# A hybrid attention trunk in float32: scratch fetches on GpSimd's DMA queue, mixer A's queries and keys a group ahead

## The chip, the cores and the metric

The kernel runs on one core of one Trainium2 chip. The metric is the device time of one execution in microseconds (us). A core has five engines with an instruction queue each: TensorE (PE, with its weight loads shown apart as PEld), VectorE (DVE), ScalarE (ACT), GpSimd (POOL) and SyncE (SP), which here only issues DMAs. An engine takes its instructions in order; one that waits holds up those behind it.

## The reference

One pre-normalised layer of a decoder trunk on 256 tokens of 4096 features. One input projection feeds two mixers and their gates. Cut to what matters here:

```
h = rmsnorm(x, norm_g);  proj = h @ w_in
(q_a, k_a, v_a, z_a, q_b, kc, vc, ksl, vsl, kwn, vwn, z_b, g_b) = split(proj)
o_a = dilated_mixture(q_a, k_a, v_a)          # 16 heads of 128; three (window, dilation) patterns
                                              # merged by their softmax denominators, ALiBi penalty
o_b = nsa(q_b, kc, vc, ksl, vsl, kwn, vwn, sigmoid(g_b))   # 16 heads; compressed, selected and
                                              # window branches, keys and values of 2 groups
y_a = rmsnorm(o_a, out_g_a) * silu(z_a)
y_b = rmsnorm(o_b, out_g_b) * silu(z_b)
out = rmsnorm(x + concat(y_a, y_b) @ w_out, final_g)
```

With 256 tokens, mixer A's three patterns of one head are one softmax over all causal keys, in which a key counts once for each pattern that holds it (the matrix MULT).

## The kernel before, in words

All products are of float32 data in split form. An operand is split into a high part, which ScalarE rounds to the matmul's type, and a low part, which VectorE takes as the difference (`split_to`, lines 102 to 109, recorded at L105 and L106, or L108 and L109 with a scale); a product is then three matmuls (`mm3`, L98 to L100). Nearly all of TensorE's time goes into the two projections.

The work comes in stages. First the input is split and three chunks of the projection (compressed, window and gate columns) are made. Then a stage of paired column chunks makes q, k, v, q_b and more with fewer products (`run_pairs`). Its results are written by GpSimd's DMAs to scratch tensors in DRAM (scr_q, scr_k, scr_v, scr_qb, scr_sel, scr_za). The **middle stage**, which the change touches, has `run_stream` work through eight more chunks: three of z_a, four of z_b, and the first of the output projection. Weights are loaded in pieces of 1 MB through SP's queue (L255), split on ACT and DVE (wh, wl) and multiplied into the accumulators acc. Between these matmuls, small steps of the attention are set: a queue `tasks` of generators, of which `advance` takes one step (to the next `yield`) each time that a credit, counted by k steps of the projection, is full. The tasks are two `compress`, four `attend_a` (mixer A, a group of four heads each), `mixer_done("a")`, `start_b`, four `attend_b`, `mixer_done("b")`, and later the turning of the gated outputs (`turn_y`, L783). After it the output projection follows in pairs, and a last stage ends the kernel.

The order of the instructions in the middle stage isn't the program's. Inside the paired stages a manual schedule keeps the order as written. Elsewhere the framework's planner orders each engine's queue: it plays the program through with its own costs, prefers what comes first in the program, and fills an engine's gaps with later work whose inputs and buffers are free by its reckoning. The chip then runs that fixed order, with semaphores for every dependence.

How data comes back from scratch: `fetch` (L562 to L565) takes a tile with the tag qk, of which there are two buffers, and issues one DMA from SP (L564). Every fetch must so wait until the tile of two fetches before has been read. In `attend_a(hg)`, before the change:

- at its start the values v and queries q of the group are there; `split_values` makes the high and low values (tile va, one of two buffers of the tag n, which kaT shares), then the keys are fetched (L639);
- `divide` (L567 to L570) scales the queries by the tokens' norm on DVE; `transposed` (L588) turns them by TensorE (L601) and splits them (qaT);
- the same for the keys (kaT); then the fetches of the next group's values and queries are issued (L649), or, in the last group, those of sel and kw, which `start_b` uses;
- a pipeline over four heads of three functions, `scores`, `turn` and `values`, two heads apart. `scores` multiplies (s, in PSUM, tag ps with three buffers), applies the distances (n, L663), takes minima (L667), exponentials (L669) and weighted sums (L670). `turn` transposes n (pt, L680) and splits it (pah on ACT, pal on DVE). `values` multiplies with va (L692, L693).

`compress(t, 1)` fetches the first group's values and queries ahead (L843). `evict_away` (L572 to L579) stores kvc, kw and vg to scratch in the first stage, from SP (L578). `mixer_done` (L728 to L759) makes the mixer's norm (rms_of; its power step runs on POOL, L115, names roa and rob), loads the stored gates z by `load` (L741, SP, four buffers of tag zt), applies SiLU and multiplies (L725). `gate_z` stores gates of chunks that come too early (L769, SP). POOL else does the small memsets of kc (L908) and c (L1038) and the stores of the paired stages.

Of the kernel before, what the change touches and what calls it, by code (L numbers as in the profile page):

```python
# [23 lines left out]
HD = 128  # L24
# [59 lines left out]
def hybrid_trunk(ctx: ExitStack, tc: tile.TileContext, a: dict):  # L84
    nc = tc.nc
# [16 lines left out]
    def split_to(h, l, src, scale=None):  # L102

        if scale is None:
            nc.scalar.activation(h, src, AF.Copy)  # L105
            nc.vector.tensor_sub(l, src, h.bitcast(F32))  # L106
        else:
            nc.scalar.activation(h, src, AF.Copy, scale=scale)  # L108
            nc.vector.scalar_tensor_tensor(l, src, scale, h.bitcast(F32), op0=OP.mult, op1=OP.subtract)  # L109
# [442 lines left out]
    st = {}  # L552
# [4 lines left out]
    def scratch(key, width=CW):  # L557
        if key not in scr:
            scr[key] = dram.tile([P, NT, width], F32, name=f"scr_{key}")
        return scr[key]  # L560

    def fetch(key, width=CW):  # L562
        t = room["zq"].tile([P, NT, width], F32, name="fetched", tag="qk", bufs=2)
        nc.sync.dma_start(t, scratch(key))  # L564
        return t  # L565

    def divide(t):  # L567

        for m in range(NT):
            nc.vector.tensor_scalar_mul(t[:, m], t[:, m], rstd[:, m : m + 1])  # L570

    def evict_away(key, width=CW):  # L572

        def done(ps):
            t = room["ev"].tile([P, NT, width], F32, name="away", tag="ev", bufs=3)
            for m in range(NT):
                nc.scalar.activation(t[:, m], ps[m][:, :width], AF.Copy, scale=rstd[:, m : m + 1])
            nc.sync.dma_start(scratch(key, width), t)  # L578
        return done  # L579

    def split_values(src):

        v = room["work"].tile([P, NT, 4, 2, HD], F32R, name="va", tag="n", bufs=2)
        for m in range(NT):
            split_to(v[:, m, :, 0], v[:, m, :, 1], src[:, m].rearrange("p (j d) -> p j d", j=4), rstd[:, m : m + 1])
        return v

    def transposed(src, key, scale=None):  # L588

        if key == "ka":  # L590
            hl = room["work"].tile([P, 2, 4, SEQ], F32R, name="kaT", tag="n", bufs=2)
            h, l = hl[:, 0], hl[:, 1]
        else:
            h = room["work"].tile([P, 4, SEQ], F32R, name=key + "Th", tag="qTh", bufs=1)
            l = room["work"].tile([P, 4, SEQ], F32R, name=key + "Tl", tag="qTl", bufs=1)
        for pair in range(2):
            pt = room["psm"].tile([P, 2, NT, P], F32, name="pt", tag="ps")
            for j in range(2):
                for m in range(NT):
                    hh = 2 * pair + j  # L600
                    nc.tensor.transpose(pt[:, j, m], src[:, m, hh * HD : (hh + 1) * HD], ident)  # L601
            split_to(h[:, 2 * pair : 2 * pair + 2].rearrange("p a b -> p (a b)"),
                     l[:, 2 * pair : 2 * pair + 2].rearrange("p a b -> p (a b)"),
                     pt.rearrange("p a b c -> p (a b c)"), scale)
            yield
        st[key + "T"] = (h, l)
# [10 lines left out]
    def o_at(which, c0, n):  # L617
        q, at = divmod(c0, DH // 2)
        return o_tiles(which)[q][:, :, at : at + n]
# [7 lines left out]
    def pipeline(units, stages, at):  # L627

        for t in range(len(units) + at[-1]):
            for f, d in reversed(list(zip(stages, at))):  # L630
                if 0 <= t - d < len(units):
                    f(units[t - d])
            yield
            yield

    def attend_a(hg):
        vsrc, qsrc = st.pop("va"), st.pop("qa")
        v = split_values(vsrc)
        ksrc = fetch(f"k{hg}")  # L639
        yield  # L640
        divide(qsrc)
        yield
        yield from transposed(qsrc, "qa", SCALE)
        yield
        divide(ksrc)
        yield
        yield from transposed(ksrc, "ka")
        if hg < 3:
            st["va"], st["qa"] = fetch(f"v{hg + 1}"), fetch(f"q{hg + 1}")  # L649
        else:  # L650
            st["sel"], st["kw"] = fetch("sel"), fetch("kw", 2 * HD)
        qh, ql = st["qaT"]
        kh, kl = st["kaT"]
        o_tiles("a")
        parts = [slice(0, P), slice(P, SPAN)]
        live = {}

        def scores(j):
            s = room["psm"].tile([P, SPAN], F32, name="s", tag="ps")
            mm3(s[:, :P], qh[:, j, :P], ql[:, j, :P], kh[:, j, :P], kl[:, j, :P])  # L660
            mm3(s[:, P:], qh[:, j, P:], ql[:, j, P:], kh[:, j], kl[:, j])
            n = room["zq"].tile([P, SPAN], F32, name="n", tag="zt", bufs=4)
            nc.vector.scalar_tensor_tensor(n, K["DA"], SLOPES[hg * 4 + j], s, op0=OP.mult, op1=OP.subtract)  # L663
            mn = room["work"].tile([P, NT], F32, name="mn", tag="mn", bufs=4)
            den = room["work"].tile([P, NT], F32, name="den", tag="den", bufs=4)
            for m in range(NT):
                nc.vector.tensor_reduce(mn[:, m : m + 1], n[:, parts[m]], axis=AX.X, op=OP.min)  # L667
            for m in range(NT):
                nc.scalar.activation(n[:, parts[m]], n[:, parts[m]], AF.Exp, bias=mn[:, m : m + 1], scale=-1.0)  # L669
                nc.vector.scalar_tensor_tensor(n[:, parts[m]], n[:, parts[m]], 1.0, K["MULT"][:, parts[m]],  # L670
                                               op0=OP.mult, op1=OP.mult, accum_out=den[:, m : m + 1])
            rden = room["work"].tile([P, NT], F32, name="rden", tag="rden", bufs=4)
            nc.vector.reciprocal(rden, den)
            live[j] = (n, rden)

        def turn(j):
            n, rden = live[j]
            pt = room["psm"].tile([P, SPAN], F32, name="pt", tag="ps")
            for b in range(3):
                nc.tensor.transpose(pt[:, b * P : (b + 1) * P], n[:, b * P : (b + 1) * P], ident)  # L680
            live[j] = (*split_psum(pt, SPAN, "pa"), rden)

        def values(j):
            ph, pl, rden = live.pop(j)
            head = hg * 4 + j

            po = room["pso"].tile([P, NT, 2, HD], F32, name="po", tag="po")
            for m, blocks in enumerate([[(0, 0)], [(P, 0), (2 * P, 1)]]):
                out = po[:, m].rearrange("p s d -> p (s d)")
                for at, b in blocks:  # L690
                    vb = v[:, b, j].rearrange("p s d -> p (s d)")
                    nc.tensor.matmul(out, ph[:, at : at + P], vb, start=b == 0, stop=False)  # L692
                    nc.tensor.matmul(out, pl[:, at : at + P], vb, start=False, stop=b == m)  # L693
            t = room["work"].tile([P, NT, 2, HD], F32, name="ot", tag="c3", bufs=1)
            for m in range(NT):
                nc.scalar.activation(t[:, m], po[:, m], AF.Copy, scale=rden[:, m : m + 1])
            nc.vector.tensor_add(o_at("a", head * HD, HD), t[:, :, 0], t[:, :, 1])

        yield from pipeline(range(4), [scores, turn, values], [0, 2, 4])
        square_sums("a", hg)  # L700

    def square_sums(which, hg):
# [26 lines left out]
    def mixer_done(which):  # L729

        rms_of(which)
        finished.add(which)
        loaded = deque()
        todo = list(waiting)
        waiting.clear()

        def load():
            z = todo.pop(0)
            sz = [room["zq"].tile([P, CW], F32, name="sz", tag="zt", bufs=4) for m in range(NT)]
            for m in range(NT):  # L740
                nc.sync.dma_start(sz[m], scratch(f"z{z[0]}{z[1]}")[:, m])  # L741
            loaded.append((z, sz))

        load()
        if todo:
            load()
        for _ in range(3):
            yield
        while loaded:
            z, sz = loaded.popleft()  # L750
            for m in range(NT):
                nc.scalar.activation(sz[m], sz[m], AF.Silu, scale=rstd[:, m : m + 1] if z == ("a", 0) else 1.0)
            yield
            yield from gate(*z, sz)
            if todo:
                load()
            yield
# [75 lines left out]
    def compress(t, which):  # L833
# [6 lines left out]
                nc.tensor.transpose(pt[:, g, m], t[:, m, c0 : c0 + HD], ident)  # L840
        nc.scalar.activation(tT, pt, AF.Copy)
        if which == 1:
            st["va"], st["qa"] = fetch("v0"), fetch("q0")  # L843
        pe, w2 = small.pop(which)
        w2h = room["work"].tile([P, 2, HD], F32R, name="w2h", tag="pTh", bufs=2)
        w2l = room["work"].tile([P, 2, HD], F32R, name="w2l", tag="pTl", bufs=2)
# [610 lines left out]
```

## Time and profile before

| | us |
|---|---|
| median of 3 runs | 1622.27 |
| lowest and highest | 1621.72, 1624.2 |
| the profiled execution | 1622.32 |
| its span, first to last instruction | 1620.5 |
| TensorE busy | 1601.9 |
| VectorE busy | 1368.8 |
| ScalarE busy | 994.6 |
| GpSimd busy | 142.6 |

The granted clock of TensorE is 0.998 of full speed. In a profile, L12 is line 12 of the kernel; an operation is named by engine, line and "out<-in" in the program's tile names; the bracket at the end of a timeline's row tells how long the engine had stood idle before it and which instruction or DMA ended that. SPq is SP's queue. A matmul row's length includes the pipeline's depth, so rows of one engine overlap. Rows of DMAs give the issue; the time to landing stands in the list of DMA issues, a median from issue to landing.

### The profile page before, as it was taken

How to read it: one execution, taken by the hardware profiler on the slowest of the kernel's cores; microseconds unless marked ns; L12 is line 12 of the kernel's file. 1: busy time of each engine (PE TensorE's matmuls, PEld its weight loads, DVE VectorE, ACT ScalarE, POOL GpSimd, SP SyncE). 2: the span in 40 equal slices, each digit the busy share in tenths (PEclk: the TensorE clock that was granted, in tenths of full speed). 3: DMA queues.
4: the chain of work that ended last, by engine and by line, in shares of the span. 5: the costliest groups of instructions: out<-in, count | busy, mean ns of one | idle time of the engine just before them, and what ended most of it. 6: DMA issues, size and time to landing. Idle time of an engine off the chain costs nothing.

```text
span 1620.5 us, 20719 instructions
## 1 busy us (share of the span) xinstructions
PE 1601.9 (99%) x7685; PEld 1326.4 (82%) x7685; DVE 1368.8 (84%) x1596; ACT 994.6 (61%) x1242; POOL 142.6 (9%) x196
## 2 busy tenths in 40 slices
PE   9999999999999999999999999999999999999997
PEld 6998888888888888888887788888888887888887
DVE  8679989898999898989878877788788779989885
ACT  7755656565656565656546666766667655656553
POOL 0000212021212020202000000000000000202110
PEclk9999999999999999999999999999999999999999
DMA  8776888888888888888888555654345556988874
GB/s 336 268 250 208 261 264 260 254 260 266 256 270 259 253 263 262 264 249 262 251 312 306 179 190 193 233 174 143 117 144 189 179 194 211 261 252 259 280 299 169
DMA packets 104565, 384.87 MB, mean 237 GB/s; under 512 B 12496, under 2 KB 13136, under 8 KB 93072
## 3 DMA queue, kind: packets, MB, share of 16 engines
q1 hardware_dynamic: 81792, 332.42, 58.3%
q0 software_dynamic: 22240, 50.08, 13.8%
q8 instruction: 60, 0.98, 0.2%
q10 hardware_dynamic: 432, 1.05, 0.2%
q14 instruction: 41, 0.34, 0.1%
HBM read 334.69 MB, written 50.91 MB: 238 GB/s over the span
## 4 chain that ended last, share of the span: by engine, by line
PE 89%; DVE 6%; issue 2%; DMA 2%; ACT 1%; SPq 0%; ACTq 0%; POOLq 0%; POOL 0%; DVEq 0%
PE p L99 16%; PE p L100 16%; PE p L98 16%; PE acc L99 9%; PE acc L100 9%; PE acc L98 9%; PE e L100 2%; PE e L98 2%; PE e L99 2%; PE ph L875 1%; DVE wl L106 1%; PE pt L1056 1%; DVE bf L443 1%; DMA w<-in_w_in 1%; DVE bp L106 1%
## 5 line engine op out<-in xcount | busy, mean ns | idle before, releaser
L106 DVE TENSOR_TENSOR wl<-w,wh 128x1024 fp32r<-128x1024 f32 (+2 forms) x178 | 207.7, 1171 | 99.4 <-ACT wh L105 98.9
L105 ACT ACTIVATE wh<-w 128x1024 fp32r<-128x1024 f32 (+2 forms) x178 | 180.4, 1017 | 115.3 <-PE acc L100 99.9
L98 PE MATMUL acc<-wh,xh 128*128 128x512 f32 (+2 forms) x640 | 242.7, 379 | 0.6 <-ACT wh L105 0.6
L443 DVE TENSOR_TENSOR bf<-bt,bf 128x2048 fp32r<-128x2048 f32 x106 | 242.1, 2284 | 0.0
L99 PE MATMUL acc<-wl,xh 128*128 128x512 f32 (+2 forms) x640 | 239.7, 375 | 1.3 <-DVE wl L106 1.3
L100 PE MATMUL acc<-wh,xl 128*128 128x512 f32 (+2 forms) x640 | 239.2, 374 | 0.0
L106 DVE TENSOR_TENSOR bp<-bw,bp 128x2048 fp32r<-128x2048 f32 x72 | 164.8, 2288 | 69.5 <-ACT bp L105 69.5
L438 ACT ACTIVATE bf<-bt 128x1024 fp32r<-128x1024 f32 x106 | 112.4, 1060 | 163.0 <-DVE bt L436 162.6
L435 ACT ACTIVATE bf<-bw 128x1536 fp32r<-128x1536 f32 x106 | 157.7, 1488 | 72.2 <-DMA bw<-in_w_in 39.4
L105 ACT ACTIVATE bp<-bw 128x2048 fp32r<-128x2048 f32 x72 | 137.6, 1911 | 94.1 <-PE e L100 78.2
L442 DVE TENSOR_TENSOR bf<-bw,bf 128x1536 fp32r<-128x1536 f32 x106 | 185.6, 1751 | 0.0
L436 DVE TENSOR_TENSOR bt<-bw 128x1024 f32<-128x1024 f32 x106 | 129.5, 1222 | 12.6 <-DMA bw<-in_w_in 7.0
L441 ACT ACTIVATE bf<-bt 128x1024 fp32r<-128x1024 f32 x106 | 112.7, 1063 | 41.8 <-DVE bt L440 38.7
L99 PEld LDWEIGHTS acc<-wl,xh 128*128 128x128 f32 x640 | 120.6, 188 | 20.1 <-DVE wl L106 3.0
L100 PEld LDWEIGHTS acc<-wh,xl 128*128 128x128 f32 x640 | 120.2, 188 | 20.4
L98 PEld LDWEIGHTS acc<-wh,xh 128*128 128x128 f32 x640 | 120.4, 188 | 18.9 <-ACT wh L105 1.1
L98 PE MATMUL p<-bp,xh 128*128 128x512 f32 x324 | 126.0, 389 | 0.0
L99 PE MATMUL p<-bp,xh 128*128 128x512 f32 x324 | 126.0, 389 | 0.0
L100 PE MATMUL p<-bp,xl 128*128 128x512 f32 x324 | 126.0, 389 | 0.0
L99 PE MATMUL p<-bf,sum 128*128 128x512 f32 x320 | 124.7, 390 | 0.0
L98 PE MATMUL p<-bf,sum 128*128 128x512 f32 x320 | 124.6, 390 | 0.0
L100 PE MATMUL p<-bf,sum 128*128 128x512 f32 x320 | 124.5, 389 | 0.0
(327 smaller groups left out, 3373.8 us busy)
## 6 DMA issues: line engine op xcount, KB each, us to landing
bw<-in_w_in SPq DMA_DIRECT2D x288, 512.0 KB, 6.5
w<-in_w_in SPq DMA_DIRECT2D x60, 1024.0 KB, 5.2
bw<-in_w_out SPq DMA_DIRECT2D x96, 512.0 KB, 5.6
w<-in_w_out SPq DMA_DIRECT2D x16, 1024.0 KB, 5.5
scr_q<-parts POOLq DMA_DIRECT2D x30, 256.0 KB, 7.8
scr_k<-parts POOLq DMA_DIRECT2D x30, 256.0 KB, 7.7
scr_v<-parts POOLq DMA_DIRECT2D x30, 256.0 KB, 7.9
scr_qb<-parts POOLq DMA_DIRECT2D x30, 256.0 KB, 8.3
```

Of the source, the lines that this page charges most:

```text
L98: nc.tensor.matmul(out, lh, rh, start=start, stop=False)
L99: nc.tensor.matmul(out, lh, rl, start=False, stop=False)
L100: nc.tensor.matmul(out, ll, rh, start=False, stop=stop)
L105: nc.scalar.activation(h, src, AF.Copy)
L106: nc.vector.tensor_sub(l, src, h.bitcast(F32))
L435: nc.scalar.activation(h[:, :3], w[:, B22:], AF.Copy)
L436: nc.vector.tensor_tensor(t[:, T3 : T1 + 1], w[:, B22 : B11 + 1], w[:, B12 : B12 + 1].to_broadcast([P, 2, CW]), op=OP.subtract)
L438: nc.scalar.activation(h[:, 3:5], t[:, T3 : T1 + 1], AF.Copy)
L441: nc.scalar.activation(h[:, 5:], t[:, T2:], AF.Copy)
L442: nc.vector.tensor_sub(l[:, :3], w[:, B22:], h[:, :3].bitcast(F32))
L443: nc.vector.tensor_sub(l[:, 3:], t, h[:, 3:].bitcast(F32))
L875: nc.tensor.matmul(ph, both, w[:, :, j], start=l == 0, stop=l == CBL - 1)
```

## The change

`fetch`, `evict_away` and the gate loads of `mixer_done` issue from GpSimd's queue instead of SP's. In mixer A, queries and keys are now what is there at a group's start. The group's values are fetched once its queries are transposed, into the queries' buffer; the next group's queries once its keys are transposed. The values are split in the fifth step of the pipeline, and behind that split the next group's keys are fetched, or sel in the last group. The yield behind the key fetch is gone and one stands behind the transposed keys, so a group still has 24 steps.

```diff
@@ fetch
-        nc.sync.dma_start(t, scratch(key))
+        nc.gpsimd.dma_start(t, scratch(key))
@@ evict_away
-            nc.sync.dma_start(scratch(key, width), t)
+            nc.gpsimd.dma_start(scratch(key, width), t)
@@ attend_a
-        vsrc, qsrc = st.pop("va"), st.pop("qa")
-        v = split_values(vsrc)
-        ksrc = fetch(f"k{hg}")
-        yield
+        qsrc, ksrc = st.pop("qa"), st.pop("ka")
         divide(qsrc)
         yield
         yield from transposed(qsrc, "qa", SCALE)
+        vsrc = fetch(f"v{hg}")
         yield
         divide(ksrc)
         yield
         yield from transposed(ksrc, "ka")
         if hg < 3:
-            st["va"], st["qa"] = fetch(f"v{hg + 1}"), fetch(f"q{hg + 1}")
+            st["qa"] = fetch(f"q{hg + 1}")
         else:
-            st["sel"], st["kw"] = fetch("sel"), fetch("kw", 2 * HD)
+            st["kw"] = fetch("kw", 2 * HD)
+        yield
@@ attend_a, its end
-        yield from pipeline(range(4), [scores, turn, values], [0, 2, 4])
+        v = None
+        for n, _ in enumerate(pipeline(range(4), [scores, turn, values], [0, 2, 4])):
+            if n == 4:
+                v = split_values(vsrc)
+                if hg < 3:
+                    st["ka"] = fetch(f"k{hg + 1}")
+                else:
+                    st["sel"] = fetch("sel")
+            yield
         square_sums("a", hg)
@@ mixer_done, load
-                nc.sync.dma_start(sz[m], scratch(f"z{z[0]}{z[1]}")[:, m])
+                nc.gpsimd.dma_start(sz[m], scratch(f"z{z[0]}{z[1]}")[:, m])
@@ compress
         if which == 1:
-            st["va"], st["qa"] = fetch("v0"), fetch("q0")
+            st["qa"], st["ka"] = fetch("q0"), fetch("k0")
```

## The prediction

> **What bounds the kernel now.** First the page's span and busy times, then the shares of the chain of waits:
>
> ```profile
> span 1620.5 us, 20719 instructions
> PE 1601.9 (99%) x7685; PEld 1326.4 (82%) x7685; DVE 1368.8 (84%) x1596; ACT 994.6 (61%) x1242; POOL 142.6 (9%) x196
> PE 89%; DVE 6%; issue 2%; DMA 2%; ACT 1%; SPq 0%; ACTq 0%; POOLq 0%; POOL 0%; DVEq 0%
> ```
>
> TensorE (PE) is busy 1601.9 of 1620.5 us and holds 89% of the chain; no queue that issues DMAs holds a share. The change leaves every matmul as it is, so it can save only time in which PE stands still, and only in the middle stage, where the fetches lie. So I asked for the waits of PE and of its weight loads (PEld) from 810 to 1320 us; columns are total us, times, longest:
>
> ```profile
> PE s L98 <- DVE pal L106: 2.8, 4, 1.1
> PE acc L99 <- DVE wl L106: 0.7, 1, 0.7
> PEld s L98 <- DVE pal L106: 3.7, 4, 1.3
> PEld s L100 <- DVE qbTl L109: 0.6, 2, 0.3
> ```
>
> That is the whole prize. Four stalls before a score matmul of mixer A, one per head group, cost 2.8 us by PE's row and 3.7 us by the weight loads', which see the wait from its start; I use 3.7. One stall at the start of the stage costs 0.7. Together 4.4 us, 0.27% of the time; about 0.2%, or 3.2 us, is what a measurement of this kernel can tell from no change.
>
> Where the four stalls come from is in the timelines of VectorE (DVE), of the DMA issues on SP and of the weight loads:
>
> ```profile
> 947.46 0.55 DVE L663 SCALAR_TENSOR_TENSOR n<-cmat,s 128x384 f32<-128x384 f32 x1 [0.33 <-PE s L100]
> 948.62 0.49 DVE L570 TENSOR_SCALAR fetched<-fetched,rstd 128x512 f32<-128x512 f32 x1 [0.61 <-DMA fetched<-scr_q]
> 949.54 0.48 DVE L570 TENSOR_SCALAR fetched<-fetched,rstd 128x512 f32<-128x512 f32 x1
> 954.56 0.55 DVE L106 TENSOR_TENSOR pal<-pt,pah 128x384 fp32r<-128x384 f32 x1
> ...
> 912.93 0.33 SPq L564 DMA_DIRECT2D fetched<-scr_q  x1
> 944.41 0.33 SPq L564 DMA_DIRECT2D fetched<-scr_q  x1
> 976.74 0.33 SPq L564 DMA_DIRECT2D fetched<-scr_q  x1
> ...
> 916.45 0.49 DVE L570 TENSOR_SCALAR fetched<-fetched,rstd 128x512 f32<-128x512 f32 x1
> 981.17 0.49 DVE L570 TENSOR_SCALAR fetched<-fetched,rstd 128x512 f32<-128x512 f32 x1 [0.83 <-DMA fetched<-scr_q]
> 1011.78 0.87 DVE L570 TENSOR_SCALAR fetched<-fetched,rstd 128x512 f32<-128x512 f32 x2
> ...
> 922.99 0.19 PEld L98 LDWEIGHTS s<-kaT,qaTh 128*128 128x128 f32 x1 [0.48 <-DVE pal L106]
> 955.16 0.19 PEld L98 LDWEIGHTS s<-kaT,qaTh 128*128 128x128 f32 x1 [1.14 <-DVE pal L106]
> 987.71 0.19 PEld L98 LDWEIGHTS s<-kaT,qaTh 128*128 128x128 f32 x1 [1.34 <-DVE pal L106]
> 1019.55 0.19 PEld L98 LDWEIGHTS s<-kaT,qaTh 128*128 128x128 f32 x1 [0.78 <-DVE pal L106]
> ```
>
> In each group the score matmul waits for a PSUM bank that DVE frees with pal, the end of a dense run of softmax work. Into that run, right behind the first n (L663), the planner has set the two divides (L570) of what was just fetched for the next group, as filler. DVE takes its instructions in order, so a fetch that lands late stops the softmax too. The first group has the divides but no wait for a fetch: stall 0.48. The second waits 0.61 more and stalls 1.14 (0.48 + 0.61 = 1.09), the third 0.83 and stalls 1.34 (sum 1.31). So a wait for a fetch at this place passes to PE one for one, while work that the planner knew of (the divides) leaves 0.48 at most. The last group divides sel and stalls 0.78.
>
> **The change part by part.** *Queues.* Some 35 DMAs leave SP for GpSimd (POOL): 20 fetches, 12 loads of gates, 3 stores. SP saves 0.33 us each by the rows above, 11.6 us in all, worth nothing: SP has no share of the chain, and in the stage PE's only wait on split weights is the 0.7. POOL gets the issues; what they cost and when they land show only in DMAs that POOL issues already:
>
> ```profile
> fetched<-scr_q SPq DMA_DIRECT2D x4, 512.0 KB, 3.8
> xr<-in_x POOLq DMA_DIRECT2D x1, 512.0 KB, 5.9
> r<-scr_r POOLq DMA_DIRECT2D x10, 256.0 KB, 8.9
> scr_r<-xr POOLq DMA_DIRECT2D x1, 512.0 KB, 2.9
> ...
> 1219.68 0.69 POOL L115 TENSOR_TENSOR rob<-rsq,nhalf 128x2 f32<-128x2 f32 x1 [25.60 <-DVE rsq L114]
> 1220.54 0.77 POOL L1122 DMA_DIRECT2D xr<-in_x  x1 [0.17 <-DMA sz<-scr_zb]
> ```
>
> A 512 KB load lands 5.9 us after issue from POOL in this very stage, against 3.8 for the queries from SP; the far ends are 8.9 (ten at once) and 2.9 (a store in a quiet moment, so a gain isn't excluded). I take 5.9, the same size, direction and stage: 2.1 us later. [...]
>
> *Mixer A's order.* The arithmetic is the same, and so are the 24 steps of a group (one yield goes with the key fetch, one comes behind the transposed keys). With two fetch buffers, the next group's queries still can't be fetched before this group's keys are transposed: the issue stays where it is (944.41 and its kin), only the landing moves. If the divides stay behind the first n, the landings at 5.9 give waits of 912.93 + 5.9 − 916.45 = 2.4 us, 944.41 + 5.9 − 948.01 = 2.3 (n ends at 947.46 + 0.55) and likewise 2.3, in place of 0, 0.61 and 0.83: 5.6 us more. If they go behind pal, all three stalls go: 0.48 + 1.14 + 1.34 = 3.0 us less. Between these ends I take 0: a planner sets the divides by the landing it assumes, and in the three rows here it missed by 0 to 0.83; I expect a like miss on the other queue. In the last group the sel divide leaves the place (sel is now fetched after the values), worth between 0.78 and 0; but the split of the values comes near the same run in all four groups:
>
> ```profile
> L109 DVE SCALAR_TENSOR_TENSOR va<-fetched,rstd,va x8: 730/743/748, 896.8 to 994.1; 128x512 fp32r<-128x512 f32 x8
> SPq L564 <- DVE va L109: 22.6, 4, 7.2
> ```
>
> Two of these, 1.49 us of DVE a group, move with two ACT copies. It is work that the planner knows of, so it cost at most 0.48 a group if it behaved as the divides did; it could also push the divides out. I set it and the sel divide against each other, 0. The keys' fetch used to wait on SP for that split (22.6 us in four); it now starts in mid-group, and its 2.1 us are hidden by the rest of the group. If that cover failed, the price would be up to 2.1 us in three groups.
>
> *The stage's start and the rest.* Rows from the waits of ACT, SP's and POOL's timelines, and the tile o_b:
>
> ```profile
> ACT w2h L105 <- DMA w<-in_cmp_k_w: 10.5, 1, 10.5
> ACT vB L105 <- DMA fetched<-scr_vg: 2.0, 1, 2.0
> ...
> 827.62 0.38 SPq L564 DMA_DIRECT2D fetched<-scr_kvc  x1
> 1210.06 9.41 SPq L741 DMA_DIRECT2D sz<-scr_zb  x4
> ...
> 832.66 0.12 POOL L908 MEMSET kc<- 128x32 f32 x1 [51.42 <-PE e L100]
> 832.98 0.58 POOL L1304 DMA_DIRECT2D scr_sel<-parts  x1 [0.19 <-issue]
> 1032.95 0.42 POOL L1038 MEMSET c<- 128x384 f32 x1 [197.79 <-DVE o_a L697]
> 173.79 2.32 POOL L461 DMA_DIRECT2D scr_q<-parts  x4 [104.40 <-ACT parts L457]
> ...
> L783 PE MATMUL pt<-ident,o_b x32: 270/272/276, 1257.7 to 1276.3; 128*128 128x128 f32 x32
> ```
>
> At the start, ACT stands 10.5 us for a small weight whose load was issued on SP just behind kvc's 512 KB. With kvc on POOL it lands earlier by some of that transfer; PE's 0.7 stall should go: −0.7. ACT waits 2.0 us for vg; up to 2.1 more, before the 0.6 us of PE waits at L100: I take +0.3, bounds 0 and 2.1. The gate loads of mixer B move behind or beside the rob step on POOL (1219.68): at worst the first starts 9.6 us later and lands 2 us later, while TensorE first turns o_b at 1257.7, some 30 us after: 0. The fetches of qb are a group ahead: 0. Of the three stores, POOL has nothing else to issue until 173.79, and kvc isn't read before 827.62: 0.
>
> The sum is −0.7 + 0 + 0 + 0.3 = −0.4 us, from 1622.32 us for the profiled execution (span 1620.5) to 1621.9. The median of three runs, 1622.27, is 0.05 below that execution, so it stands for the median too.
>
> **The rivals.** *Gain in full:* the divides land behind pal, the sel divide goes, the split values find room. Then 3.7 + 0.7 go: 1617.9. For it: a later landing can drive the filler out of the dense run, and the keys come early. Against: n to pal lasts 7 us (947.46 to 954.56), longer than the 2.1 us by which the landing moves, so the next gap may still be inside it.
>
> *Slower: DVE stops for the later landing.* The divides, or the split values, keep their place. Three waits of 2.3 to 2.4 add 5.6, vg 2.1, the start gives 0.7 back: +7.0, so 1629.3. It decides from a landing later than the assumed one by 1.1 us more than now in each of the three groups (3.2 us in all). For it: the one-for-one rows. [...]
>
> *Slower: POOL's queue.* POOL also takes its work in order; a fetch set behind the memset of c, which stood 197.79 us, or behind rob, starts late. Against: the planner put the memset of kc ahead of stores that come first in the program, so it places by readiness. If it hits one fetch by 7 us with 2 us of cover, +5: 1627.
>
> *The change misses its aim:* SP's queue was never what starved PE, so freeing it does nothing. This is part of my forecast.
>
> **How the numbers follow.** Forecast 0.46 (its own range 1619.1 to 1625.5, all within 0.2%); gain in full 0.26; DVE stops 0.22; POOL's queue 0.06. Rounded: faster 0.26, the same 0.46, slower 0.28. To hold 8 in 10 the range reaches just past the full gain, 1617.5, and up to 1629.0, near the price of the stopped DVE; above it lie the rest of that case and of POOL's, at most 0.15.
>
> **What would show it.** In the changed profile: TensorE's waits of s for pal (3.7 by the weight loads) tell the sum at once; the idle before L570 "<-DMA fetched" and its place against n and pal tell which case it is; POOL's fetches should land in about 5.9 us; PE's stall at the stage's start should be gone; ACT's wait for vg should be 2 to 4 us. The prediction is wrong if PE's stalls in the stage fall below 1.5 us or pass 8, or if the time moves by more than PE's stalls do.

## The result and the profile after

| | before | after |
|---|---|---|
| median, us | 1623.09 (4 runs) | 1641.59 (4 runs) |
| lowest and highest | 1621.72, 1624.2 | 1640.98, 1644.33 |
| the profiled execution | 1622.32 | 1640.98 |
| its span | 1620.5 | 1639.2 |

The change makes the kernel slower: the ratio is 1.0118, with a 95% interval of 1.01 to 1.0135. The forecast was 1621.9 with a range up to 1629.0, so it was wrong by 19.7 us and outside its range.

The page of after, its busy times and the chain of waits:

```profile
PE 1608.1 (98%) x7685; PEld 1331.1 (81%) x7685; DVE 1369.0 (84%) x1596; ACT 995.3 (61%) x1242; POOL 161.6 (10%) x231
PE 82%; issue 7%; DVE 6%; DMA 3%; ACT 1%; POOL 0%; POOLq 0%; ACTq 0%; SPq 0%; DVEq 0%
```

The matmuls are the same 7685, yet TensorE's busy time rises from 1601.9 to 1608.1 us: some of them have become longer. The chain gives PE 82% where it had 89%. Issue, time in which the engine on the chain waited for nothing that the profile shows, has 7% where it had 2%; why was not worked out. POOLq, the issuing of DMAs on GpSimd, has no share. So no wait for GpSimd to issue shows on the chain; the next places to look are the landings, and something that makes matmuls slow.

The waits of TensorE in the middle stage (810 to 1340 us), then those of VectorE and ScalarE that stand behind them (total us, times, longest):

```profile
PE pt L679 <- DVE n L669: 7.9, 6, 2.0
PE acc L99 <- DVE wl L106: 4.9, 1, 4.9
PE pt L1063 <- DVE nb L1029: 2.5, 1, 2.5
PE s L98 <- DVE pal L106: 2.2, 2, 1.4
...
DVE va L109 <- ACT va L108: 8.7, 3, 2.9
DVE fetched L570 <- DMA fetched<-scr_q: 7.9, 1, 7.9
DVE fetched L570 <- DMA fetched<-scr_qb: 2.5, 2, 2.2
...
ACT va L108 <- DMA fetched<-scr_v: 8.6, 3, 2.9
```

The old stalls of s for pal, most of the prize of the prediction, have shrunk from 2.8 to 2.2 us. Three new kinds have come. **In three of the four groups** ScalarE waits 2.9 us for the values' fetch before it can split them; VectorE, whose half of the split needs ScalarE's, waits as long; and TensorE then stands before the transposes of the probabilities n. **At the stage's start** one divide waits 7.9 us for the first queries, and TensorE stands 4.9 us for split weights. **In mixer B** a divide waits for qb, and TensorE 2.5 us for nb.

The middle stage's values, in the timelines of SP, GpSimd, ScalarE, VectorE and TensorE of after (second group):

```profile
946.20 0.33 SPq L255 DMA_DIRECT2D w<-in_w_in  x1
...
946.04 0.54 POOL L564 DMA_DIRECT2D fetched<-scr_v  x1 [21.89 <-PE pt L601]
...
952.33 1.34 ACT L108 ACTIVATE va<-fetched,rstd 128x512 fp32r<-128x512 f32 x2 [2.85 <-DMA fetched<-scr_v]
...
953.09 1.42 DVE L109 SCALAR_TENSOR_TENSOR va<-fetched,rstd,va 128x512 fp32r<-128x512 f32 x2 [2.88 <-ACT va L108]
...
955.79 0.68 DVE L106 TENSOR_TENSOR kaT<-pt,kaT 128x512 fp32r<-128x512 f32 x1
956.39 0.55 DVE L662 SCALAR_TENSOR_TENSOR n<-cmat,s 128x384 f32<-128x384 f32 x1
...
958.33 0.30 PE L679 MATMUL pt<-ident,n 128*128 128x128 f32 x1 [0.77 <-DVE n L669]
960.58 0.44 PE L679 MATMUL pt<-ident,n 128*128 128x128 f32 x2 [1.95 <-DVE n L669]
```

The planner has set the split of the values ahead of the second half of the keys (kaT at 955.79) and of the first n, not in the middle of the heads as the program has it. The fetch is issued at 946.04 and must land before 949.48 (952.33 − 2.85) to cost nothing; that is 3.4 us. It takes 6.3. Everything behind it on ScalarE and VectorE is late by 2.9, and TensorE stands 0.77 + 1.95 = 2.7 us.

Why 6.3? The DMA queues of after in two stretches, before and behind 948.8 (packets, MB, share of 16 engines), and the two issues of the first:

```profile
q1 hardware_dynamic: 48, 0.39, 43.2%
w<-in_w_in SPq DMA_DIRECT2D x1, 1024.0 KB, 5.8
fetched<-scr_v POOLq DMA_DIRECT2D x1, 512.0 KB, 6.3
...
q1 hardware_dynamic: 96, 0.66, 43.2%
q0 software_dynamic: 152, 0.56, 41.2%
```

q1 carries what SP issues, q0 what GpSimd issues: by the two pages, 14.26 MB move from q1 (332.42 to 318.16) to q0 (50.08 to 64.34) with the change. From 946 to 948.8 only the weights move, though they were issued 0.16 us after the values. From 948.8 on both move side by side until both are there at about 952: 0.66 MB of weights and the values' half MB. A piece of 1 MB that nobody needs yet has gone along with the half MB that ScalarE waits for.

The last unforeseen thing is in the windows of after (start:end and length in us, PE busy with its count of matmuls, granted clock PEclk, DMA share, GB/s):

```profile
842.31:845.73 3.42, 0.00 (x0) 1.00 0.99 408
845.73:849.14 3.41, 3.24 (x8) 0.50 0.69 233
...
958.37:961.78 3.41, 1.46 (x10) 1.00 0.63 259
961.78:965.19 3.41, 3.41 (x12) 0.50 0.25 62
...
992.50:995.91 3.41, 0.89 (x4) 1.00 0.98 404
995.91:999.32 3.41, 3.18 (x12) 0.50 0.04 12
...
1030.05:1033.46 3.41, 2.19 (x14) 1.00 0.43 168
1081.25:1084.66 3.41, 0.86 (x8) 1.00 0.14 60
1084.66:1088.07 3.41, 3.41 (x13) 0.50 0.00 0
```

Behind each of four long stalls the granted clock is 0.50 for exactly one window of 3.41 us. PE is "busy" there and does little more than half as much (in the second of the four, 128x512 matmuls start 0.43 us apart, at 962.21, 962.64 and 963.07; behind it 0.24, at 966.01, 966.24 and 966.48); that is the rise of its busy time. By the granted clock each such window costs about 3.41 x 0.50 = 1.7 us, an estimate, the four 6.8. Before had none in the stage: its clock reads 1.00 in every stretch of 50 us from 810 on.

The account, by the spans and busy times of the two pages: of the 18.7 us by which the span grows, 6.2 are longer busy time of TensorE (1608.1 − 1601.9), which fits the clock's 6.8, and 12.5 are more idle time (31.1 us in place of 18.6). The rows of waits above say much the same: 17.5 us, where before has 4.0 in the same view.

### The profile page after: what moved, and what is told of

It reads as the page before. It is cut to its first block, busy times and chain, and to the rows that moved or that the text cites. A ratio compares the mean times of both kernels' runs of the same rounds, so it can differ in the third digit from the quotient of the medians.

```text
span 1639.2 us, 20717 instructions
## 1 busy us (share of the span) xinstructions
PE 1608.1 (98%) x7685; PEld 1331.1 (81%) x7685; DVE 1369.0 (84%) x1596; ACT 995.3 (61%) x1242; POOL 161.6 (10%) x231
## 3 DMA queue, kind: packets, MB, share of 16 engines
q1 hardware_dynamic: 76752, 318.16, 55.2%
q0 software_dynamic: 26256, 64.34, 16.2%
## 4 chain that ended last, share of the span: by engine, by line
PE 82%; issue 7%; DVE 6%; DMA 3%; ACT 1%; POOL 0%; POOLq 0%; ACTq 0%; SPq 0%; DVEq 0%
PE p L99 16%; PE p L100 16%; PE p L98 16%; PE acc L99 7%; PE acc L98 7%; PE acc L100 7%; PE e L99 2%; PE e L100 2%; PE e L98 2%; DMA fetched<-scr_v 1%; DVE wl L106 1%; PE ph L882 1%; PE pt L1063 1%; DVE bf L443 1%; DMA w<-in_w_in 1%
```

## The experiments

The theories named in the expectations: **Order**, the new order of mixer A's steps is what costs; **Queue**, that the DMAs go through GpSimd; and, once the first runs were read, **Rings**, a sharper form of Queue: a fetch on GpSimd has lost its place ahead of a weight load on SP that is released at nearly the same time, so it shares the DMA engines with that megabyte. All ratios are to the kernel before, run on the same chip, with 95% intervals; times of two different experiments come from different chips in part, so small differences between them are not read.

**The new order, all DMAs on SP** (in the changed kernel):

```
-        nc.gpsimd.dma_start(...)      # fetch, evict_away, load
+        nc.sync.dma_start(...)
```

> The changed order of mixer A with every DMA left on SP. Theory Order (the planner sets the split of the values, and the divide of the first queries, where their fetch has not landed; in-order ACT and DVE stop, PE follows): the place of these instructions is nearly that of the changed kernel, so most of the loss stays: 1632 to 1642 us, ACT waits of 1 to 3 us for scr_v in three groups, half-speed clock windows after long stalls. Theory Queue (the landing from GpSimd's queue is what is late): loss gone, 1620 to 1625 us.

Measured: 1623.05 against 1623.11, ratio 0.9999 (0.9989 to 1.0008). The longest of its waits of TensorE:

```profile
PE s L98 <- DVE pal L106: 3.3, 4, 1.2
```

The second group's fetch of values with the weight load behind it, and ScalarE's split, in the timelines:

```profile
940.66 0.33 SPq L564 DMA_DIRECT2D fetched<-scr_v  x1
941.19 0.33 SPq L255 DMA_DIRECT2D w<-in_w_in  x1
...
943.87 0.60 ACT L105 ACTIVATE kaT<-pt 128x512 fp32r<-128x512 f32 x1 [0.75 <-PE pt L601]
944.37 1.33 ACT L108 ACTIVATE va<-fetched,rstd 128x512 fp32r<-128x512 f32 x2
```

And that fetch in the list of DMA issues:

```profile
fetched<-scr_v SPq DMA_DIRECT2D x1, 512.0 KB, 3.3
```

Order, as a cause by itself, falls. The values' split stands at the same place, right behind the first half of kaT, but the fetch lands in 3.3 us with the weights behind it in one queue; the split's row has no wait at all. The new order by itself gains nothing either: the four old stalls cost 3.3 in place of 2.8.

At the stage's start the planner itself acts on the queue. On SP, q0's fetch stands behind loads of weights and is issued at 845.51; the divide is set late (854.92), waits 0.7 us there, and no stall of TensorE follows. On GpSimd it is issued at 832.95 and the planner sets its divide ahead of the weights' splits:

```profile
832.95 0.56 POOL L564 DMA_DIRECT2D fetched<-scr_q  x1 [0.18 <-issue]
...
841.56 0.88 DVE L570 TENSOR_SCALAR fetched<-fetched,rstd 128x512 f32<-128x512 f32 x2 [7.92 <-DMA fetched<-scr_q]
...
844.63 3.49 DVE L106 TENSOR_TENSOR wl<-w,wh 128x1024 fp32r<-128x1024 f32 x3
...
845.90 0.79 PE L99 MATMUL acc<-wl,xh 128*128 128x512 f32 x1 [4.93 <-DVE wl L106]
```

These are rows of after's timelines. From 832.95 to 840 the DMA engines were full (82.8% with q1, 16.3% with q0); the fetch took 8.5 us, and a divide that nobody needed yet held up the splits of the weights behind it.

**The queue alone** (in the kernel before):

```
-        nc.sync.dma_start(...)        # fetch, evict_away, load
+        nc.gpsimd.dma_start(...)
```

> The kernel before with only the queue changed (fetches, evictions, gate loads from GpSimd). Theory Order: 1621 to 1626 us, the three waits of the queries' divides within 1 us of those before. Theory Queue: the divides wait 2.3 us each, 1629 us or more.

Measured: 1635.59, ratio 1.0072 (1.0057 to 1.0087). Two of its divides in the timeline of VectorE, in the third group behind the first n, in the fourth ahead of the second half of the keys:

```profile
984.61 0.48 DVE L570 TENSOR_SCALAR fetched<-fetched,rstd 128x512 f32<-128x512 f32 x1 [3.75 <-DMA fetched<-scr_q]
1015.87 0.49 DVE L570 TENSOR_SCALAR fetched<-fetched,rstd 128x512 f32<-128x512 f32 x1 [4.35 <-DMA fetched<-scr_sel]
```

In the old order the new queue costs 12.5 us; the profiled execution has a granted clock of 0.994, as in after, where before has 0.998. By these rounded clocks 0.003 to 0.005 of its span of 1634.1 us, 5 to 8 us, are the clock's, an estimate. Behind these two waits TensorE stands 2.4 and 3.3 us. It is here that the prediction's rival with the stopped DVE can be seen in its own place: waits of 3.75 and 4.35 us, where it had worked out 2.3 to 2.4.

**Hold the first queries' divide** (in the changed kernel): its factor is made from a late value of the second `compress`, times 0, plus rstd, so that the planner can't set it early.

```
+    def held_rstd(name, after):
+        r = cst.tile([P, NT], F32, name=name)
+        nc.vector.scalar_tensor_tensor(r, after, 0.0, rstd, op0=OP.mult, op1=OP.add)
+        return r
-        divide(qsrc)
+        divide(qsrc, None if hg else st["rq"])     # st["rq"] = held_rstd("rq", x[:, :, 0])
```

> The changed kernel, with the divide of the first group's queries made to wait for a late step of the second compress (its scale is that step's output times 0 plus rstd, one small DVE instruction). Theory Order: the stall of about 5 us at 841 us and the half-speed clock window behind it (3.4 us at half speed, 1.7 us lost) go: 1633 to 1636 us; the stalls in the groups stay. Theory Queue: the wait only moves to the next fetch, 1638 us or more.

Measured: 1634.73, ratio 1.0071 (1.0054 to 1.0088), 6.9 us less than after. The stall of 4.9 is gone; with the window at half clock behind it in after, estimated at 1.7, that makes 6.6. ScalarE's waits for the values stay (8.7 us in three). The start's stall is so shown to come from that divide. The likeness of 6.6 and 6.9 is partly luck: other stalls moved too, and the granted clock of the profiled execution is 0.996, where after has 0.994.

**Hold the split of the values as well**, until the third head's denominators:

```
-                v = split_values(vsrc)
+                v = split_values(vsrc, held_rstd(f"rv{hg}", live[2][1]))
```

> As the run that holds the first divide, and the split of each group's values too is made to wait for the third head's softmax denominators (same device). Theory Order: the three waits of ACT for scr_v go as well, with the stalls of 3 us and two half-speed windows behind them: 1621 to 1627 us. Theory Queue: other fetches still land late, above 1630 us.

Measured: 1630.05, ratio 1.0041 (1.0027 to 1.0056). It missed what was expected. The waits for scr_v are gone, and other instructions take their place. Its longest wait of TensorE, then one of VectorE:

```profile
PE s L98 <- DVE pal L106: 5.2, 4, 1.8
...
DVE fetched L571 <- DMA fetched<-scr_q: 2.0, 3, 1.3
```

The split of the values is no longer in the run ahead of the first pal: in the first group it starts at 931.05, behind two pal (924.84 and 926.41). So it isn't filler ahead of pal, as the prediction had feared. There stand the divides of the next queries (918.55), the first with a wait of 1.25 us for its fetch, and splits of weights. Why the stalls of s for pal have grown to 5.2 us was not worked out further.

**Values on SP again** (in the changed kernel):

```
+        queue = nc.sync if key in ("v0", "v1", "v2", "v3") else nc.gpsimd
+        queue.dma_start(t, scratch(key))
```

> The changed kernel, with only the four value fetches of mixer A back on SP. Theory Rings (a fetch from GpSimd issued together with a weight load from SP reaches the DMA engines behind that load's 1 MB, where from SP it went ahead of it): scr_v lands 3.3 to 4 us after issue instead of 6.3, ACT's three waits of 2.9 us go, with three stalls of 3 us and two windows at half clock: 1628 to 1633 us; the 5 us stall at the stage's start and the one near 1081 stay. Rival Path (every fetch from GpSimd lands late, whatever runs beside it): the next fetches take over the waits, 1636 us or more.

Measured: 1635.1 (1632.81 to 1641.02), ratio 1.0078 (1.0056 to 1.01). The four fetches of values land in 3.4 us (median) and ScalarE has no wait for them left, as Rings says; the median lies 6.5 us below after and 2.1 above the range that was given for Rings, short of the rival's 1636. The start's stall stays (5.2 us), and the granted clock of the profiled execution is 0.996, where before has 0.998.

**Also the first queries and qb on SP**:

```
+        queue = nc.sync if key in ("v0", "v1", "v2", "v3", "q0") or key[:2] == "qb" else nc.gpsimd
```

> As the run with the values on SP, and the first queries and mixer B's queries are back on SP too; the keys, the later queries, sel, kw, vg, kvc, the gates and the stores stay on GpSimd. Theory Rings: only fetches that met a weight load were costly, so this is back at the kernel before, 1621 to 1626 us, with no window at half clock in the stage. Rival Path: 1628 us or more.

Measured: 1630.73, ratio 1.0038 (1.0025 to 1.0052), a miss. The landings of its fetches, in the list of DMA issues:

```profile
fetched<-scr_k POOLq DMA_DIRECT2D x4, 512.0 KB, 6.2
fetched<-scr_q SPq DMA_DIRECT2D x1, 512.0 KB, 8.8
```

And a wait of TensorE:

```profile
PE ph L883 <- DVE bhl L106: 2.4, 1, 2.4
```

The first queries take 8.8 us from SP too (9.3 in the first experiment, 8.5 from GpSimd in after): at the start the landing is late from either queue. Issued at 844.27 in place of 832.95, they no longer hold up the splits of the weights, but their divide still waits 1.7 us ahead of bhl; TensorE stands 2.4 us for that. The granted clock of the profiled execution is 0.996. And once the worst fetches are back, those left on GpSimd seem to meet weights in their turn: the keys, which landed in 4.6 in after, now take 6.2, and their divides wait 2.9 us in two. So which fetch is hit seems to depend on what is issued beside it, not on the fetch. How the 7 us that are left divide was not worked out.

**The weights on GpSimd too** (the changed kernel, with the stage's weight loads in the same queue as its fetches):

```
+            queue = nc.gpsimd if room.get("mid") else nc.sync     # the middle run_stream
+            queue.dma_start(t, src)
```

> The changed kernel, with the weight loads of the middle stage moved to GpSimd's queue as well, so that fetch and weights share one queue and keep the order of issue; the values' fetch stands ahead of the weight load in three groups. Theory Rings: scr_v lands within 4.5 us in those groups although it comes from GpSimd, ACT waits less than 1 us each, two or three stalls of 3 us go; 1626 to 1634 us if the weights themselves aren't late. Rival Path: scr_v still lands at 6 us and ACT waits 2 to 3 us, 1640 us or more.

Measured: 1632.42, ratio 1.0047 (1.0032 to 1.0061). Its GpSimd timeline in the second group:

```profile
947.84 0.54 POOL L565 DMA_DIRECT2D fetched<-scr_v  x1 [7.37 <-PE pt L602]
948.46 0.54 POOL L256 DMA_DIRECT2D w<-in_w_in  x1
```

And the landings of the four fetches of values, from the list of DMA issues:

```profile
fetched<-scr_v POOLq DMA_DIRECT2D x4, 512.0 KB, 3.7
```

This is the test that parts Rings from a slow GpSimd: the values still go through GpSimd, with the weights now 0.62 us behind them in one queue, and land in 3.7 us in place of 6.3; ScalarE's wait for them, 8.6 us in after, is not among its rows of 1.3 us and more, and VectorE's for ScalarE's half is 1.1 in all, in place of 8.7. What remains is mostly the start: there VectorE waits 7.5 us for scr_q, and TensorE up to 4.5 in one stall, as in after; the granted clock of the profiled execution is 0.996.

**The kernel before, with the next group's query divides and the divides of sel held** until the fourth head's denominators (`held_rstd` as above):

```
+            if j == 3:
+                st["rq"] = held_rstd(f"rq{hg}", rden)
-        divide(qsrc)
+        divide(qsrc, st.get("rq"))
-        divide(sel)
+        divide(sel, st["rq"])
```

> The kernel before, with the divide of the next group's queries (and of sel) made to wait for the fourth head's softmax denominators, so that it leaves the dense run of VectorE between the first n and the first pal. If those divides and their wait for the fetch cause the four stalls of 3.7 us, these fall below 1.5 us: 1618 to 1622 us. If another term holds pal back, nothing changes: 1622 to 1624 us.

Measured: 1618.9, ratio 0.9967 (0.9954 to 0.9979): faster than both kernels. TensorE's waits for pal:

```profile
PE s L98 <- DVE pal L106: 0.8, 4, 0.2
```

They were 2.8. The divides were the cause of the four stalls, as the prediction read it. Of the 3.4 us by which the span falls, this row accounts for 2.0; where the rest comes from was not traced.

**Only the stores and the gate loads on GpSimd** (in the kernel before; fetches on SP):

> The kernel before with only the three stores of the first stage and the gate loads of the mixers' ends issued from GpSimd; the fetches stay on SP and in their old order. Theory Rings (only a fetch that somebody waits for within some microseconds, and that is released together with a 1 MB load of weights, costs anything): nothing here is such a fetch, so 1621.5 to 1625 us and a ratio of 0.999 to 1.001, with the gate loads landing later than before without a wait on TensorE. Its rival, that any DMA moved from SP to GpSimd costs, gives a third or so of the 12.5 us that the queue's change alone cost, so 1626 to 1629.

Measured: 1626.53, ratio 1.0016 (1.0008 to 1.0025), 2.6 us by the ratio. That is outside what Rings had said and, as a time, inside its rival's range. GpSimd's timeline at the end of mixer A:

```profile
1034.46 0.42 POOL L1038 MEMSET c<- 128x384 f32 x1 [198.13 <-DVE o_a L697]
1035.37 1.19 POOL L741 DMA_DIRECT2D sz<-scr_za  x2 [0.50 <-PE acc L100]
```

And ScalarE's waits:

```profile
ACT sz L752 <- DMA sz<-scr_za: 4.2, 3, 2.2
```

The gates of mixer A now stand behind the memset of c, and that waits for the last heads; in the kernel before SP issued the first of them at 1028.50, 4.4 us ahead of that memset (1032.95). ScalarE then waits 4.2 us for them with the next weights' split behind it. The gates' loads land in 4.1 us (median), as from SP in the kernel before (4.0). So by these rows it is neither a shared megabyte nor a price on any moved DMA, but in-order issue on a queue that had something else to do; no run takes the memset out of the way to show it.

**The new order on SP, with the same divides held** as in the eighth:

> The changed kernel's order with all DMAs back on SP, and the next group's query divides (and the divides of sel) held until the fourth head's denominators. By the reading of the four stalls before the score matmuls (filler set in the dense run of softmax work), the 3.3 us of waits of s for pal fall to about 1.8, as in the same edit of the kernel before, and the time to 1618 to 1621 us. If in this order the split of the values, which now lies in the middle of the run, holds the place of the divides, the waits stay near 3 and the time at 1622 to 1624.

Measured: 1620.44, ratio 0.9977 (0.9968 to 0.9986). Three of the four stalls go and one of 1.7 us stays; the granted clock of the profiled execution is 0.997. It beats both kernels. Whether the old order with the same edit is better still isn't shown: the two intervals overlap.

## Why the prediction was wrong, point by point

*What bounds the kernel* was right, and so was the source of the four stalls: the eighth experiment took the divides away from that place and got faster. That *SP's relief is worth nothing* was right too: the first experiment, which gives all issues back to SP, runs in the same time as before.

*The step that failed first is the price of a landing.* The prediction took one landing for each queue, 5.9 us for GpSimd by the row of xr, 3.8 for SP, and counted the 2.1 between. There is no such number, for either queue. From the lists of DMA issues, first of before, then two of after:

```profile
fetched<-scr_v SPq DMA_DIRECT2D x4, 512.0 KB, 5.6
...
fetched<-scr_q POOLq DMA_DIRECT2D x4, 512.0 KB, 3.9
fetched<-scr_v POOLq DMA_DIRECT2D x4, 512.0 KB, 6.3
```

Before, the values took 5.6 us from SP, beside the 3.8 of q that the prediction used. In after the fetches of q take 3.9 and that of sel 3.6 from GpSimd, those of v 6.3 in the median, and the first q 8.5. For the values, the seventh experiment shows that what decides is the megabyte that travels at the same time (3.7 us with it behind them in one queue). The stretches of after show the two side by side, 0.66 and 0.56 MB from 948.8 on, and with that a cost that the prediction did not draw: a queue is also a place ahead of others, and leaving it gave the values' fetch 6.3 us instead of the 3.3 of the first experiment. With that, the terms of the sum that failed are the split of the values and the fetches of qb, both set at 0, the start, set at −0.7, and the clock, which had none.

*The split of the values* was set at no more than 0.48 us a group as "work that the planner knows of", and then, against the sel divide, at 0. The instructions are such work, but they now stand behind a fetch issued a few microseconds earlier, and that wait had no term. The prediction asked what each moved instruction costs, and not whether its input is there where the planner sets it. It measured 2.9 us on ScalarE and VectorE in three groups, 2.7 of it on TensorE in the group shown; over the three groups the wait for n is 7.9.

*The divides of q* it set at 0, with 5.6 us as the upper end. Inside the groups that was right: after has one single wait for scr_q, and it is the start's. The reason was another than the one given: the landing of q did not move (3.9 us against 3.8), so there was nothing for the planner to allow for.

*The start*, −0.7, was half right. With kvc off SP, ScalarE's wait before w2h fell from 10.5 to 8.0, as it said, though the next one, for the same weights, rose from 2.1 to 3.6. But a fetch that is issued earlier also let the planner set its divide earlier, and that cost 4.9 us and a window at half clock. *The keys' cover* held (GpSimd's keys land in 4.6, nobody waits over 0.7). *The vg* term was small, as said: ScalarE waits 1.8 us for it, a little under the 2 to 4 that were forecast. *qb at 0* was wrong: 2.5 us. The fetch concerned is the third of qb. It lands in 6.5 us in after and took 5.8 from SP before; but its divide, which ran 7.1 us behind the issue before (1057.26 to 1064.34), is ready at 1078.03, 4.4 us behind it (1073.67), because the planner has set it ahead of two steps of nb that it followed before. So here too an earlier place of the consumer counts, more than the landing.

*The gates at 0* is put in doubt by the ninth experiment, which moves them together with the three stores. The prediction looked at mixer B's gates only; mixer A's stand behind the memset of c, a place that its own third rival had named for fetches. In after that memset is as late (the gates wait for it too), but no stall of TensorE stands there.

*The clock* had no term at all: 6.8 us. In after it fell to 0.50 for one window of 3.41 us behind four of the stalls, and the window ahead of such a drop needn't be idle throughout (PE was busy 1.46 of 3.41 us in one).

*The rivals.* The nearest was the stopped DVE, 1629.3, with the sign and, by its words "or the split values", the place right. It was 12 us short: its waits were priced with the 2.1, and the start and the clock were not in it. That GpSimd itself is slow isn't seen: its issues of fetches last 0.54 to 0.56 us in the rows above, and with the weights in the same queue the values' fetch lands in 3.7. The sign that the prediction named for itself, "if the time moves by more than PE's stalls do", is what happened: 12.5 us more of idle time, 18.7 of span. So is the other, stalls of more than 8 us: the four rows of waits shown above sum to 17.5.

What stays open: how the 12.5 us of the queue alone divide among its fetches was worked out only for the two waits above, and three buffers for fetched, which could let the values be fetched before the keys, were not tried.

## What to carry to other kernels

A queue is an order: before moving a small, awaited load to another queue, look which large load is issued next to it, and count the time in which both share the engines (here 6.3 us to land in place of 3.3). Where a planner fills in-order engines, an earlier issue isn't an earlier landing (the values, issued 0.16 us ahead of the weights, landed 0.3 behind them), and it can draw the consumer ahead of work that is needed first (the first queries' divide, for which TensorE stood 4.9 us); hold filler by a dependence on the work that it shall follow (here 4.7 us gained on the old kernel). And a stall on a busy TensorE can cost a half-clock window on top: in after, stalls of 2.5 to 4.9 us had one behind them in four places, about 1.7 us each, and one of 2.4 in a fifth had none.

## What the runs showed of the hardware

The drop of the clock. In after, the window behind one in which PE was busy 0.00, 0.86, 0.89 or 1.46 of 3.41 us ran at 0.50; behind 1.96 (1033.46 to 1036.87) and 2.19 it ran at 1.00. The busy times are those of modelled ends of matmuls, so the border between 1.46 and 1.96 is approximate. No drop in after lasted two windows.

The starts of the windows at half clock in after (845.73, 961.78, 995.91, 1084.66) are 34, 10 and 26 times 3.413 us apart, so in this trace they fit one grid whatever the stall's own time: the fourth group's stall of the same kind, at 1028 to 1031, fell across two windows of it (busy 2.21 and 2.19) and lost no clock. Which of these stalls cost 1.7 us more is then, as the author reads it, partly chance of position. The tenth experiment's runs fit that: six with a mean granted clock of 0.997 took 1620.4 to 1621.7 us, five with 0.998 took 1618.0 to 1619.5.

GpSimd's fetches: in the second group of after, the values' first packet left 2.8 us after issue, behind a weight load issued 0.16 us after it on SP, whose first packet left 1.0 us after its issue. For the first group's values, issued at 915.57 with no weight load issued between 912.09 and 920.76, it was 1.25, and they landed in 3.8.
